# The closing norm of the last 256 rows of a decoder step: its parts moved between VectorE, ScalarE and TensorE

## The chip, the cores and the metric

The kernel runs on one core of one Trainium2 chip. The metric is the device time of one execution in microseconds (us); the median of the runs counts. TensorE (PE) multiplies matrices, VectorE (DVE) and ScalarE (ACT) work element by element, SyncE (SP) issues the transfers (DMA). All matrix results land in PSUM, which has eight banks here; VectorE and ScalarE read them from there.

## The reference, cut to what matters

One layer of a decoder over 528 prompt rows (16 of them learned tokens that are dropped at the end) and 8 sample rows, 2048 columns, float32. The change touches only the last line, the closing norm:

```python
def layer_norm(x, g, b):
    mu = jnp.mean(x, -1, keepdims=True)
    var = jnp.mean(jnp.square(x - mu), -1, keepdims=True)
    return (x - mu) * lax.rsqrt(var + LN_EPS) * g + b
...
    a = silu(h1 @ w_gate) * (h1 @ w_up)
    ff = a @ w_down
    return layer_norm(DEEPNORM_ALPHA * h1 + ff, ln2_g, ln2_b)
```

The outputs of this part are 512 prompt rows (`yp`) and 8 sample rows (`ys`). Weight `ln2_g` and bias `ln2_b` are rows of 2048 values, the same for every row of the output.

## The kernel before, in words

Every weight is split into two float32r parts (`split`, L187 on ScalarE and L188 on VectorE), and every product is three matrix multiplications (`products`, L203, L204, L206). Nearly the whole kernel is such products. The last stage, around which the change lies, holds the residual sum transposed: `acc[m]`, m = 0 to 15, is a tile of 128 columns of the model by 520 rows (8 sample rows, then 512 prompt rows).

The last stage runs over two halves of the rows, h = 0 (sample rows and prompt rows 0 to 255) and h = 1 (prompt rows 256 to 511), and in each over the 16 column tiles m. `down(h, m)` (L1320 to L1333) loads weights (half 0 only, a load for four m at a time, into one of two buffers, L1325), multiplies into a PSUM bank in 12 matrix multiplications, and VectorE adds the bank onto `acc[m]` (L1333). Banks come in turn from a ring of eight.

Class `Rows` (L1338) holds 128 prompt rows; there are four objects, called r0 to r3 below. `Rows.part(q)` (from L1343) runs after each fourth m: TensorE turns four 128x128 tiles into one bank `tz` (L1347), ScalarE copies the bank to a tile `z` of 128 rows by 512 columns (L1349), and VectorE takes its statistics (L1351, for the last quarter from the bank itself). `Rows.end` (from L1354) joins the four statistics (L250), makes the inverse standard deviation with one square root on ScalarE and a Newton step on VectorE (`rstd_of`, L236 to L242), and then makes two passes over each quarter: L1358 subtracts the mean and multiplies by the weight, L1360 multiplies by the inverse deviation and adds the bias, and L1361 sends the quarter out. `ends` hands these passes of r0 and r1 out, one or two per m, during half 1; those of r2 and r3 follow after the last product. `sample_rows` (L1364 to L1409) is the same norm for the 8 sample rows, in six steps put between the products by `next(sample)` in L1411 to L1431; its last step sends 16 small pieces out through SP (L1408).

The order of the instructions on each engine is made by the framework's planner, which simulates the program with its own costs and lets an instruction go when what it needs is there in that simulation; each engine then works off its list in that order. Two helpers bind the planner: `step(engine)`, a block whose instructions on that engine come after those of the `step` block before it, and `tc.high_priority`, used for the weights. In the kernel before, nothing in the last stage stands in a `step` block.

## Time and profile before

| | us |
|---|---|
| median of 3 runs | 1931.51 |
| lowest and highest run | 1930.22, 1931.68 |
| profiled execution: span from its first to its last instruction | 1931.1 |
| TensorE busy in it | 1894.4 (98%) |
| VectorE busy in it | 1539.9 (80%) |
| ScalarE busy in it | 944.1 (49%) |
| granted TensorE clock, mean over the span | 0.992 |

The profile is of one execution, of which the span is the time listed; it lies within the range of the runs and 0.4 us below their median. Times in the rows further down are microseconds from the start of that span; the ones that matter here lie between 1885 and 1931.

### The profile page before, as it was taken

To read this page: it belongs to the slowest core of one execution; us is meant where nothing else is said; L and a number is where in the kernel's file an instruction comes from. 1 tells how busy PE (TensorE), PEld (TensorE's weight loads), DVE (VectorE), ACT (ScalarE), POOL (GpSimd) and SP (SyncE) were. 2 spreads that over 40 slices of the span, in tenths; PEclk is the share of its full clock that TensorE was granted. 3 is DMA by queue.
4 is the path that set the end of the run, shared out by engine and by line. 5 is a ranking of instruction groups with operands and counts; after the bars stand their busy time and mean duration, and the time that the engine had idled before them with its cause. 6 is when DMAs were issued, how large, how long until landed. Compare 5 with 4: busy or idle time off the path is not lost.

```text
span 1931.1 us, 39334 instructions
## 1 busy us (share of the span) xinstructions
PE 1894.4 (98%) x15533; PEld 1865.8 (97%) x15533; DVE 1539.9 (80%) x2734; ACT 944.1 (49%) x1808; POOL 2.7 (0%) x9
## 2 busy tenths in 40 slices
PE   9999999999999999999999999999999999999996
PEld 8999999999989999999999999999999999999996
DVE  6666667768777888888888888888877888888878
ACT  6644445545654544554455555555554444344341
POOL 0000000000000000000000000000000000000000
PEclk9999999999999999999999999999999999999998
DMA  8732222665744555454545445454469664645332
GB/s 276 233 101 66 71 78 75 211 202 193 250 150 164 160 160 172 142 162 158 175 139 178 141 138 165 146 167 145 164 212 356 214 221 162 223 163 202 94 99 89
DMA packets 145241, 319.28 MB, mean 165 GB/s; under 512 B 14288, under 2 KB 66232, under 8 KB 144952
## 3 DMA queue, kind: packets, MB, share of 16 engines
q1 hardware_dynamic: 144480, 315.71, 49.7%
q8 instruction: 122, 2.00, 0.4%
q10 hardware_dynamic: 576, 1.05, 0.2%
q14 instruction: 63, 0.52, 0.1%
HBM read 265.22 MB, written 54.03 MB: 165 GB/s over the span
## 4 chain that ended last, share of the span: by engine, by line
PE 92%; DVE 4%; ACT 2%; DMA 1%; issue 1%; SPq 0%; DVEq 0%; ACTq 0%
PE p_g L203 7%; PE p_g L204 7%; PE p_g L206 7%; PE p_u L203 7%; PE p_u L206 7%; PE p_u L204 7%; PE tri L203 7%; PE tri L206 7%; PE tri L204 7%; PE o L203 3%; PE o L206 3%; PE o L204 3%; PE p_u L996 2%; PE mm_u L203 2%; PE mm_u L206 2%; PE mm_u L204 2%
## 5 line engine op out<-in xcount | busy, mean ns | idle before, releaser
L187 ACT CAST rr<-fr 128x512 fp32r<-128x512 f32 (+1 forms) x1056 | 658.0, 643 | 776.6 <-DVE fr L196 224.0
L188 DVE TENSOR_TENSOR rr<-fr,rr 128x512 fp32r<-128x512 f32 (+1 forms) x1056 | 738.0, 717 | 264.5 <-ACT rr L187 253.2
L196 DVE TENSOR_TENSOR fr<-fr 128x1024 f32<-128x1024 f32 (+1 forms) x304 | 319.7, 1052 | 5.8 <-DMA fr<-in_w_g_dram 5.0
L203 PE MATMUL p_g<-rr 128*128 128x260 f32 x830 | 235.5, 285 | 7.4 <-ACT rr L187 7.1
L206 PE MATMUL p_g<-rr 128*128 128x260 f32 x830 | 230.6, 282 | 0.0
L204 PE MATMUL p_g<-rr 128*128 128x260 f32 x788 | 221.8, 282 | 0.0
L203 PE MATMUL p_u<-rr 128*128 128x260 f32 x770 | 217.5, 283 | 0.2 <-ACT rr L187 0.2
L206 PE MATMUL p_u<-rr 128*128 128x260 f32 x770 | 215.3, 282 | 0.0
L204 PE MATMUL p_u<-rr 128*128 128x260 f32 x748 | 210.6, 282 | 0.0
L206 PE MATMUL tri<-rr 128*128 128x260 f32 x696 | 196.8, 283 | 1.5 <-DVE rr L188 1.5
L203 PE MATMUL tri<-rr 128*128 128x260 f32 x696 | 197.0, 283 | 0.7 <-ACT rr L187 0.7
L204 PE MATMUL tri<-rr 128*128 128x260 f32 x696 | 196.7, 283 | 0.0
L203 PEld LDWEIGHTS p_g<-rr 128*128 128x128 f32 x830 | 156.2, 188 | 9.9 <-ACT rr L187 9.4
L206 PEld LDWEIGHTS p_g<-rr 128*128 128x128 f32 x830 | 155.2, 189 | 0.0
L204 PEld LDWEIGHTS p_g<-rr 128*128 128x128 f32 x788 | 148.1, 188 | 0.0
L203 PE MATMUL o<-rr 128*128 128x260 f32 x512 | 145.0, 284 | 0.3 <-ACT rr L187 0.3
L203 PEld LDWEIGHTS p_u<-rr 128*128 128x128 f32 x770 | 144.9, 188 | 0.3 <-ACT rr L187 0.3
L206 PEld LDWEIGHTS p_u<-rr 128*128 128x128 f32 x770 | 144.6, 189 | 0.0
L204 PE MATMUL o<-rr 128*128 128x260 f32 x512 | 144.1, 282 | 0.0
L206 PE MATMUL o<-rr 128*128 128x260 f32 x512 | 143.6, 282 | 0.2 <-DVE rr L188 0.2
L204 PEld LDWEIGHTS p_u<-rr 128*128 128x128 f32 x748 | 140.6, 188 | 0.0
L206 PEld LDWEIGHTS tri<-rr 128*128 128x128 f32 x696 | 131.3, 189 | 2.2 <-DVE rr L188 2.2
(320 smaller groups left out, 4570.0 us busy)
## 6 DMA issues: line engine op xcount, KB each, us to landing
fr<-in_w_u_dram SPq DMA_DIRECT2D x100, 512.0 KB
fr<-in_w_g_dram SPq DMA_DIRECT2D x90, 512.0 KB
fr<-in_w_d_dram SPq DMA_DIRECT2D x64, 640.0 KB
t_d<-fr SPq DMA_DIRECT2D x140, 260.0 KB
fr<-in_w_o_dram SPq DMA_DIRECT2D x64, 512.0 KB
fr<-in_w_in_dram SPq DMA_DIRECT2D x48, 512.0 KB
rr<-t_d SPq DMA_DIRECT2D x87, 260.0 KB
mid_b<-t_d SPq DMA_DIRECT2D x53, 260.0 KB
```

The costliest lines, as they stand in the source:

```text
L187: nc.scalar.copy(wh, s)
L188: last_lo[0] = (lo or nc.vector).tensor_sub(wl, s, wh.bitcast(F32)).ins
L196: i = op(*args).ins
L203: nc.tensor.matmul(o, wh, hi[j], start=first, stop=False, skip_group_check=onto)
L204: nc.tensor.matmul(o, wh, lo[j], start=False, stop=False, skip_group_check=onto)
L206: nc.tensor.matmul(o, wl, hi[j], start=False, stop=last, skip_group_check=onto)
L996: nc.tensor.matmul(bk, self.q(0, n - 1)[:, k * P:(k + 1) * P], z1[0][4 * (n - 1) + k // 2][:, k % 2, :], start=(k == 0), stop=(k == 7))
```

## The change

For the last 256 rows (r2 and r3, now objects of class `Last`) the norm is rearranged. With s the inverse deviation, the output is z·g·s − mean·s·g + b. For columns 0 to 1535 the product z·g is made as soon as a quarter is there (`Last.scale`), and the rest, −mean·s·g + b, comes from one small TensorE product per quarter (`five`, `lw`, `rows5`: five rows to the product, which are two numbers per row and their low-order parts), and one VectorE pass, after the statistics are known, joins the two. The last quarter keeps its two passes (`centre`, `affine`). The statistics of the first three quarters come from sums that ScalarE accumulates while it copies (`Identity`) and squares (`Square`); only the last quarter keeps `bn_stats`, in two halves. The turning of `acc[m-1]` now stands inside `down(1, m)`, after three of its four groups of products. For r0 and r1, one of two passes per quarter moves to ScalarE (`activation` with scale and bias), and VectorE multiplies and adds. `affine_rows` prepares weight and bias rows for the small products during half 0. The steps of the sample rows come earlier. What follows the last product is bound in `step` blocks. The number of `z` buffers goes from 19 to 16, one for each quarter of r0 to r3, so none is used twice.

```diff
--- before.py
+++ after.py
@@ -47,7 +47,7 @@
 NRAW = 5
 NT = 3
 NG = 56
-NZ = 19
+NZ = 16
 FRW, RRW, MDW = 18960, 24368, 9880
 WIDTH = {"pts": 512, "wh": 512, "wl": 512}
 
@@ -1317,7 +1317,7 @@
     sp[:] = [Pool(rr), KT]
     WIDTH.update(wh=512, wl=512)
 
-    def down(h, m):
+    def down(h, m, mid=None):
 
         if m % 4 == 0 and h == 0:
             pw[h] = plp.tile([P, 4, 4, P], F32, tag="pl", name=f"pl{h}_{m}", bufs=2)
@@ -1330,6 +1330,8 @@
         wh, wl = ws[m]
         for f in range(4):
             products([out], wh[:, f, :], wl[:, f, :], [ah[f][:, hs]], [al_[f][:, hs]], f == 0, f == 3)
+            if f == 2 and mid:
+                mid()
         nc.vector.tensor_add(acc[m][:, hs], acc[m][:, hs], out)
 
     gb = [[pb.tile([P, 512], F32, name=f"gb{i}_{q}") for q in range(4)] for i in range(2)]
@@ -1354,10 +1356,14 @@
         def end(self):
             n = self.n
             mu, r = stats_end(pb, self.st, self.mv, n, f"z{self.c0}")
+            nmr = pb.tile([P, 1], F32, name=f"nmr{self.c0}")[:n]
+            nc.vector.scalar_tensor_tensor(nmr, mu, -1.0, r, op0=ALU.mult, op1=ALU.mult)
+            for z in self.z:
+                nc.scalar.activation(z, z, AF.Identity, scale=r, bias=nmr)
             for q, z in enumerate(self.z):
-                nc.vector.scalar_tensor_tensor(z, z, mu, gb[0][q][:n], op0=ALU.subtract, op1=ALU.mult)
+                nc.vector.tensor_mul(z, z, gb[0][q][:n])
                 yield
-                nc.vector.scalar_tensor_tensor(z, z, r, gb[1][q][:n], op0=ALU.mult, op1=ALU.add)
+                nc.vector.tensor_add(z, z, gb[1][q][:n])
                 nc.sync.dma_start(self.dst[:, q * 512:(q + 1) * 512], z)
                 yield
 
@@ -1408,27 +1414,159 @@
             nc.sync.dma_start(ys[:, m * P:(m + 1) * P], zo[x * NS:(x + 1) * NS])
         yield
 
+    class Last:
+
+        def __init__(self, c0, i, dst):
+            self.c0, self.i, self.dst, self.z = c0, i, dst, []
+            self.st = sts[:, i]
+            self.nc = pb.tile([P, 1], F32, name=f"nc_z{c0}")
+
+        def turn(self, m):
+            q, i = divmod(m, 4)
+            if i == 0:
+                self.tp = bank(f"tz{self.c0}_{q}", 512)
+            nc.tensor.transpose(self.tp[:, i * P:(i + 1) * P], acc[m][:, self.c0:self.c0 + P], ident)
+            if q == 3:
+                if i % 2:
+                    nc.vector.bn_stats(self.st[:, 3 + i // 2, :], self.tp[:, (i - 1) * P:(i + 1) * P])
+            elif i == 3:
+                z = zp.tile([P, 512], F32, tag="z", name=f"z{self.c0}_{q}", bufs=NZ)
+                nc.scalar.activation(z, self.tp, AF.Identity, accum_out=sums[:, self.i, q, 0:1])
+                if q == 0:
+                    nc.scalar.activation(self.nc, sums[:, self.i, 0, 0:1], AF.Copy, scale=-1.0 / 512)
+                nc.scalar.activation(junk, z, AF.Square, bias=self.nc, accum_out=sums[:, self.i, q, 1:2])
+                self.z.append(z)
+
+        def sums_end(self):
+            s1, s2 = [sums[:, self.i, :, k:k + 1] for k in range(2)]
+            d = pb.tile([P, 3, 1], F32, name=f"d_z{self.c0}")
+            both = lambda x: x.to_broadcast([P, 3, 2])
+            nc.vector.tensor_scalar(d, s1, 1.0 / 512, self.nc, op0=ALU.mult, op1=ALU.add)
+            nc.vector.tensor_mul(d, d, d)
+            nc.vector.scalar_tensor_tensor(d, d, -512.0, s2, op0=ALU.mult, op1=ALU.add)
+            nc.vector.tensor_scalar(self.st[:, 0:3, 1::3], both(s1), 1.0 / 512, None, op0=ALU.mult)
+            nc.vector.tensor_scalar(self.st[:, 0:3, 2::3], both(d), 0.5, None, op0=ALU.mult)
+
+        def scale(self, q):
+            nc.vector.tensor_mul(self.z[q], self.z[q], gb[0][q])
+
+    def last_rows(part):
+
+
+        mv = pb.tile([P, 2, 2], F32, name="mv_l")
+        for x in part:
+            nc.vector.bn_aggr(mv[:, x.i, :], x.st.rearrange("p a b -> p (a b)"))
+        mu, var = mv[:, :, 0], mv[:, :, 1]
+        ve, r, t = [pb.tile([P, 2], F32, name=f"{n}_l") for n in ("ve", "r", "t")]
+        zl = [zp.tile([P, 512], F32, tag="z", name=f"z{x.c0}_3", bufs=NZ) for x in part]
+
+        dve = nc.vector
+        wide = lambda a: a.rearrange("p (a b) -> p a b", b=1).to_broadcast([P, 2, 3])
+
+        def centre(x):
+            dve.scalar_tensor_tensor(zl[x.i], x.tp, mu[:, x.i:x.i + 1], gb[0][3], op0=ALU.subtract, op1=ALU.mult)
+
+        def put_out(x, q, z):
+            nc.sync.dma_start(x.dst[:, q * 512:(q + 1) * 512], z)
+
+        def affine(x):
+            with step(dve):
+                dve.scalar_tensor_tensor(zl[x.i], zl[x.i], r[:, x.i:x.i + 1], gb[1][3], op0=ALU.mult, op1=ALU.add)
+            put_out(x, 3, zl[x.i])
+
+        with step(dve):
+            dve.tensor_scalar(ve, var, EPS, None, op0=ALU.add)
+            nc.scalar.activation(t, ve, AF.Sqrt)
+        with step(dve):
+            centre(part[0])
+        with step(dve):
+            dve.reciprocal(r, t)
+            dve.tensor_mul(t, r, r)
+            dve.tensor_mul(t, t, ve)
+            dve.tensor_scalar(t, t, -0.5, 1.5, op0=ALU.mult, op1=ALU.add)
+            dve.tensor_mul(r, r, t)
+        affine(part[0])
+        with step(dve):
+            dve.scalar_tensor_tensor(five[:, :, 0:3], wide(mu), -1.0, wide(r), op0=ALU.mult, op1=ALU.mult)
+        with step(dve):
+            centre(part[1])
+        affine(part[1])
+        tt = bank("five", 2 * P)
+        with step(nc.tensor):
+            for x in part:
+                nc.tensor.transpose(tt[:5, x.i * P:(x.i + 1) * P], five[:, x.i, :], ident)
+        nc.scalar.copy(lh, tt[:5])
+        with step(dve):
+            dve.scalar_tensor_tensor(lw, lh.bitcast(F32), nident[:5, 2:3], tt[:5], op0=ALU.mult, op1=ALU.add)
+
+        pieces = [(x, q) for q in range(3) for x in part]
+        bk = [bank(f"sh{x.i}_{q}", 512) for x, q in pieces]
+
+        for n, (x, q) in enumerate(pieces):
+            with step(nc.tensor):
+                nc.tensor.matmul(bk[n], lw[:, x.i * P:(x.i + 1) * P], rows5[:, q * 512:(q + 1) * 512], start=True, stop=True)
+            with step(dve):
+                dve.scalar_tensor_tensor(x.z[q], x.z[q], r[:, x.i:x.i + 1], bk[n], op0=ALU.mult, op1=ALU.add)
+            put_out(x, q, x.z[q])
+
     sample = sample_rows()
     next(sample)
-    rows = [Rows(NS + P * i, P, yp[P * i:P * (i + 1), :]) for i in range(4)]
-    for h, part in ((0, rows[:2]), (1, rows[2:])):
-        for m in range(KT):
-            down(h, m)
-            if h == 1:
-
-                for _ in range(2 if m % 4 == 1 else 1):
-                    next(ends, None)
-            if h == 0 and m in (1, 2):
-                for i, q in gb_loads[4 * m - 4:4 * m]:
-                    nc.sync.dma_start(gb[i][q], ln2gb[i:i + 1, q * 512:(q + 1) * 512].to_broadcast([P, 512]))
-            if m % 4 == 3:
-                for x in part:
-                    x.part(m // 4)
-            if (h, m) in ((0, 4), (0, KT - 1), (1, 4), (1, 10), (1, KT - 1)):
-                next(sample)
-        ends = chain.from_iterable([x.end() for x in part])
-    for _ in ends:
+    five = pb.tile([P, 2, 5], F32, name="five")
+    nc.gpsimd.memset(five, 1.0)
+    nident = pb.tile([P, 8], F32, name="nident")
+    nc.scalar.activation(nident, ident[:, 0:8], AF.Copy, scale=-1.0)
+    mask = pb.tile([P, 1], F32, name="mask")
+    nc.vector.tensor_add(mask, nident[:, 1:2], nident[:, 4:5])
+    lp = Pool(rr)
+    lh = lp.tile([5, 2 * P], F32R, name="lh")
+    lw = lp.tile([5, 2 * P], F32R, name="lw")
+    rows5 = lp.tile([5, D], F32R, name="rows5")
+
+    def affine_rows(q):
+        sl = slice(q * 512, (q + 1) * 512)
+        g5 = pb.tile([5, 512], F32, name="g5", bufs=1)
+        h5 = lp.tile([5, 512], F32R, name="h5", bufs=1)
+        nc.sync.dma_start(g5[0:3], ln2gb[0:1, sl].to_broadcast([3, 512]))
+        nc.sync.dma_start(g5[3:5], ln2gb[1:2, sl].to_broadcast([2, 512]))
+        nc.scalar.copy(h5, g5)
+        nc.vector.scalar_tensor_tensor(rows5[:, sl], h5.bitcast(F32), mask[:5], g5, op0=ALU.mult, op1=ALU.add)
+
+    sts = pb.tile([P, 2, 5, 6], F32, name="sts")
+    sums = pb.tile([P, 2, 3, 2], F32, name="sums")
+    nc.gpsimd.memset(sts, 256.0)
+    junk = zp.tile([P, 512], F32, name="junk")
+    rows = [Rows(NS + P * i, P, yp[P * i:P * (i + 1), :]) for i in range(2)]
+    last = [Last(NS + P * i, i - 2, yp[P * i:P * (i + 1), :]) for i in (2, 3)]
+    for m in range(KT):
+        down(0, m)
+        if m in (1, 2):
+            for i, q in gb_loads[4 * m - 4:4 * m]:
+                nc.sync.dma_start(gb[i][q], ln2gb[i:i + 1, q * 512:(q + 1) * 512].to_broadcast([P, 512]))
+        if m in (6, 8, 10, 12):
+            affine_rows(m // 2 - 3)
+        if m % 4 == 3:
+            for x in rows:
+                x.part(m // 4)
+        if m in (4, KT - 1):
+            next(sample)
+    ends = chain.from_iterable([x.end() for x in rows])
+    for m in range(KT):
+        down(1, m, lambda: [x.turn(m - 1) for x in last if m])
+        for _ in range(2 if m % 4 == 1 else 1):
+            next(ends, None)
+        if m % 4 == 2 and m > 2:
+            for x in last:
+                x.scale(m // 4 - 1)
+        if m == 14:
+            for x in last:
+                x.sums_end()
+        if m in (3, 7, 11):
+            next(sample)
+    for _ in chain(ends, sample):
         pass
+    for x in last:
+        x.turn(KT - 1)
+    last_rows(last)
 
 
 # ---- launch: one core; the arrays are laid out for the loads, the values are those that come in ----
```

## Rows read from the trace of the kernel before

**Rows 1.** The page, part 1: busy time, share and instructions by engine.
```profile
PE 1894.4 (98%) x15533; PEld 1865.8 (97%) x15533; DVE 1539.9 (80%) x2734; ACT 944.1 (49%) x1808; POOL 2.7 (0%) x9
```
**Rows 2.** Three stretches: us, busy time (instructions) of each engine, granted clock, DMA share, GB/s.
```profile
core 0: us, PE busy (x) PEld busy (x) DVE busy (x) ACT busy (x) POOL busy (x), PEclk, DMA share, GB/s
1885.05:1911.70 26.65, 26.65 (x231) 26.65 (x230) 22.00 (x59) 5.54 (x12) 0.00 (x0) 1.00 0.23 81
1911.70:1915.50 3.80, 1.01 (x10) 0.77 (x8) 3.74 (x12) 2.05 (x4) 0.00 (x0) 0.99 0.00 0
1915.50:1931.10 15.60, 0.45 (x1) 0.18 (x1) 11.88 (x31) 0.67 (x3) 0.00 (x0) 0.50 0.39 139
```
**Rows 3.** Timeline of TensorE at its end: start, busy us, instruction, count [idle before <-releaser].
```profile
1911.33 0.28 PE L206 MATMUL d<-rr 128*128 128x256 f32 x1
1911.45 1.25 PE L1347 MATMUL tz<-fr 128*128 128x128 f32 x10
1915.91 0.45 PE L1403 MATMUL to<-fr 128*128 128x128 f32 x1 [3.21 <-DVE fr L236]
```
**Rows 4.** Timeline of VectorE from the last addition on, and its issues on SP.
```profile
1911.65 0.42 DVE L1333 TENSOR_TENSOR fr<-fr,d 128x256 f32<-128x256 f32 x1 [0.89 <-PE d L206]
...
1915.25 0.38 DVE L250 BATCH_NORM_AGGREGATE fr<-fr 128x2 f32<-128x24 f32 x2
...
1915.74 2.73 DVE L1358 SCALAR_TENSOR_TENSOR mid_c<-mid_c,fr 128x512 f32<-128x512 f32 x4
1918.39 0.14 DVE L236 TENSOR_SCALAR fr<-fr 128x1 f32<-128x1 f32 x1
...
1921.23 0.28 DVE L239 TENSOR_TENSOR fr<-fr 128x1 f32<-128x1 f32 x2
...
1922.00 5.38 DVE L1360 SCALAR_TENSOR_TENSOR mid_c<-mid_c,fr 128x512 f32<-128x512 f32 x8
...
1925.60 2.14 SPq L1361 DMA_DIRECT2D out_dram<-mid_c  x4
```
**Rows 5.** Timeline of VectorE, 1872 to 1877: the unit prices.
```profile
1872.61 1.28 DVE L1351 BATCH_NORM_STATS2 fr<-mid_c 128x6 f32<-128x512 f32 x2
1873.80 0.41 DVE L1333 TENSOR_TENSOR fr<-fr,d 128x264 f32<-128x264 f32 x1
1874.13 1.89 DVE L188 TENSOR_TENSOR rr<-fr,rr 128x512 fp32r<-128x512 f32 x3
1875.94 0.42 DVE L1333 TENSOR_TENSOR fr<-fr,d 128x264 f32<-128x264 f32 x1
```
**Rows 6.** Timeline of VectorE, early in half 1.
```profile
1888.88 0.70 DVE L1351 BATCH_NORM_STATS2 fr<-tz 128x6 f32<-128x512 f32 x1 [1.14 <-ACT mid_c L1349]
...
1891.03 0.10 DVE L236 TENSOR_SCALAR fr<-fr 128x1 f32<-128x1 f32 x1
1891.04 2.73 DVE L1358 SCALAR_TENSOR_TENSOR mid_c<-mid_c,fr 128x512 f32<-128x512 f32 x4
1893.69 0.15 DVE L236 TENSOR_SCALAR fr<-fr 128x1 f32<-128x1 f32 x1
...
1896.39 0.16 DVE L238 RECIPROCAL fr<-fr 128x1 f32<-128x1 f32 x1
...
1897.32 0.15 DVE L238 RECIPROCAL fr<-fr 128x1 f32<-128x1 f32 x1
```
**Rows 7.** ScalarE, groups by line and shape: count, busy us, mean ns, idle before.
```profile
L341 ACT ACTIVATE fr<-fr,mid_a 128x512 f32<-128x512 f32 x16 | 12.1, 805 | 2.5 <-DVE mid_a L336 2.5
L570 ACT ACTIVATION_READ_ACCUMULATOR mid_a<-mid_a,fr 128x1 f32 x64 | 12.0, 187 | 0.0
L1349 ACT COPY mid_c<-tz 128x512 f32<-128x512 f32 x16 | 8.6, 590 | 11.6 <-PE tz L1347 11.6
```
**Rows 8.** ScalarE and SP timelines, weights of the last eight m of half 0.
```profile
1862.16 5.74 SPq L1325 DMA_DIRECT2D fr<-in_w_d_dram  x8
...
1868.86 2.19 ACT L187 CAST rr<-fr 128x512 fp32r<-128x512 f32 x4 [3.14 <-DMA fr<-in_w_d_dram]
```

## The prediction

> **What bounds the kernel now.** I read the page first, then the last stretch in three windows, then the lists of TensorE and VectorE in order of time. The page has TensorE busy for 98% of the span [rows 1], so a change in the last stage is worth only what it does to the end. In the windows [rows 2] the reader is to see three regimes. Up to 1911.7 us TensorE is busy without a gap, but VectorE is busy 22.0 of 26.65 us beside it: it is nearly full too. From 1911.7 on TensorE has ten turns left [rows 3], and VectorE alone sets the end: it is busy 3.74 of 3.80 us, then 11.88 of the last 15.6, and stops at 1927.4 [rows 4] (1922.00 + 5.38). The rest, 1931.1 − 1927.4 = 3.7 us, is the last transfers. So the end is reached when VectorE has worked off its list, and the question is how much work the change takes from that list, and how much waiting it puts in.
>
> **Unit prices on VectorE**, as the distance from one start to the next [rows 5]: statistics of 128x512, 1.19 / 2 = 0.60 us; a product or sum of two 128x512 tiles, 1.81 / 3 = 0.60; the addition of a bank of 256 columns, 0.33. A two-operation pass with a per-row scalar is 2.65 / 4 = 0.66 [rows 6]. A step of the Newton chain that waits for the step before it takes about 0.2: four steps of two instructions each fill 1921.23 to 1922.00 [rows 4], 0.77 / 4 = 0.19.
>
> **r0 and r1 in half 1.** Now: after the mean is known, eight passes of L1358 run at once from 1891.04 while the square root is on its way; the reciprocals come at 1896.39 and 1897.32, behind those passes [rows 6]. In the change both VectorE passes need ScalarE's pass, which needs the inverse deviation. So VectorE has nothing of r0 and r1 to do until: end of the second "add eps", pulled up to about 1891.15, + square root and handing over 0.35 + reciprocal and four steps 1.0 + the negated mean 0.2 + ScalarE's first 128x512 pass, 0.805 [rows 7] (an activation with the same two per-row operands) + 0.2 for hand-overs = **1893.7**. Early bound 1893.0 (no hand-over seen); late bound 1898.5: the reciprocals stay where the planner put them, 1896.39 + 1.2 + 0.8. I take 1893.7, since what held them back, the eight passes, is gone. The passes themselves are 16 x 0.60 instead of 16 x 0.66.
>
> **VectorE from 1893.7 to its last addition.** 16 passes of r0, r1: 9.65. Additions m = 4 to 14: 11 x 0.33 = 3.6. Sample rows, all of them now before the end: three passes of 128x128 and one difference, two sums, six small steps, 1.7 (half of that stood here before). Six weight passes of `scale`: 6 x 0.60 = 3.6. `sums_end`, ten tiny instructions: between 0.7 (0.07 each, packed) and 2.0 (0.2 each, waiting); 1.2, since there is other work to put between. Two half statistics: 2 x 0.33 = 0.7. Removed here are four statistics of 128x512 (2.4), the other four were after the last product. Sum 20.5 us, so the last addition would start at 1893.7 + 20.5 = **1914.2**. Its bank is ready earlier: eight of the ten turns now stand ahead of the last products instead of behind them, 8 x 0.11 = 0.9, so the last multiplication starts at 1911.33 + 0.9 = 1912.2 [rows 3] and the bank is there at 1912.55. VectorE is 1.65 us behind TensorE there; before it was waiting, 0.89 us [rows 4].
>
> **From the last addition to VectorE's end.** Addition 0.42; two turns and hand-overs 0.5; two half statistics 0.66; joining 0.36 [rows 4] (0.38 for two); add eps 0.1; `centre` of r2 0.66, which covers the square root; reciprocal and four steps 1.0; `affine` of r2 0.66; the entries of `five` 0.2; `centre` and `affine` of r3 1.33, which just cover two slow turns of `five` (0.45 each at half clock [rows 2, 3]) and ScalarE's copy; `lw` 0.4; first small product 0.6; six last passes 6 x 0.663 = 3.98. Sum 10.9, against 1927.4 − 1911.65 = 15.75 now. The small products after the first are hidden: 512 columns at the clock of 0.50 that the last window grants are about 0.48 us (four times the 0.12 between the starts of 256 columns at full clock, 1911.33 and 1911.45 [rows 3]), under 0.66. The reads from PSUM cost no more in the rows: statistics from `tz` and from `z` both take 0.69 or 0.70.
>
> **Sum.** 1914.2 + 10.9 = 1925.1 for VectorE, 2.3 before 1927.4; the transfers behind it keep their 3.7, since they again follow passes 0.66 apart. Span 1928.8, and with the 0.4 between the profile's span and the median, **1929.2 us**. As a check by work alone: −4.8 (eight statistics) −10.6 (16 passes) −1.0 (two chains) −1.0 (cheaper passes) + 1.3 + 3.6 + 1.2 + 6.6 (ten passes at the end) + 1.8 (chain, `five`, `lw`) = −2.9, and idle time +2.4 (1.3 early, 1.1 at the end) −1.6 (the gaps of now) gives −2.1.
>
> **Costed at nothing.** ScalarE: eight passes at 0.70 to 0.80, six copies and six squares at 0.6 to 0.8 with 0.19 for each sum [rows 7], some 18 us of the 23 from 1889; the last squares end near 1911, and the joining waits for them only at 1915.4. If that cover goes, each us late is a us. SP: the sample pieces leave earlier, so they no longer stand between the last rows' issues. Half 0: four preparations of 0.6 on ScalarE and 0.66 on VectorE, and eight small loads on SP. Each load but the first pair waits for the preparation before it, and behind it on SP stand the weight loads of 1862.16 [rows 8], the last of which ScalarE already waits for, 3.14 us; TensorE wants that weight at about 1871.8 (eight m of 12 multiplications at 0.12 and 16 turns at 0.11 before half 0 ends at 1885.05); its split is done near 1870.3 (1868.86 plus both parts, some 0.7 each), 1.5 us ahead. Under that, nothing; over it, TensorE stops.
>
> **A bank with two readers.** The row at 1888.88 shows VectorE idle for 1.14 us until ScalarE had copied the same bank, although neither needs the other [rows 6]. In the change the last quarter's four turns and two half statistics share a bank, so the turn of `acc[14]` waits for the first half statistics, with three multiplications of m = 15 behind it. The Trainium skill, "PSUM — Partial Sum Buffer", section "PSUM bank collisions raise a hardware error", says the same as a rule: guard by bank, not by address. By that rule TensorE could stop here, where the change's columns alone would let it go on.
>
> **Rivals.** (1) VectorE is not behind: the planner finds the work room, and the last addition starts at 1912.55. Then 1923.45 + 3.7 + 0.4 = **1927.5**. For it: the idle 0.5 and 0.6 us at the end could take the last `scale` passes, which stand in no `step`. Against it: the list of 20.5 us. (2) The other side: the reciprocals keep their places, the first product comes at 1898.5. Five additions, a sum and a difference fit into the wait (1.7), so the last addition starts at 1898.5 + 18.8 = 1917.3, the end is 1917.3 + 10.9 + 3.7 + 0.4 = **1932.3**, slower. It decides from a first product later than about 1897.5. For it: 5.4 us between L236 and L238 in the list now. (3) The shared bank: if the planner puts the first half statistics last before the addition, at 1914.2, then the two turns and three multiplications and the bank's hand-over come after it, about 1 us: **1930.2**. (4) SP: a preparation load holds the weights up 1.5 us and more; each further us is one, say 3: **1932.2** or above. (5) The change doesn't do what it says: `scale` is made early in the code, but its passes run after the last product. As VectorE's list is full, the sum stays, 1929.2, less up to 1.1.
>
> **Chances.** Forecast 0.47 (with (5)), (1) 0.22, (2) 0.16, (3) 0.08, (4) 0.07. A measurement of this kernel tells 0.2%, 3.9 us, from no change: faster means below 1927.6, slower above 1935.4. (1) lies at that line and the forecast's early edge touches it: 0.20. Slower needs (2) or (4) and more: 0.07. The range leaves out the extremes of (1) and (4): 1926.8 to 1932.9.
>
> **What would show it.** Right: eight of the ten turns stand before the last multiplication; VectorE's first product for r0 at about 1893.7, its last addition late, at 1914 with no wait before it; 10 to 11 us from there to the last pass; 3.7 after. Wrong: a VectorE that waits for TensorE before the last addition (rival 1), a reciprocal beyond 1896 (rival 2), any gap on TensorE between 1870 and 1912 (rivals 3 and 4), or squares on ScalarE after 1914.

## The result and the profile after

The changed kernel takes 1935.12 us, median of 20 runs (1932.08 to 1937.49), against 1931.98 for the kernel before, of which 20 more runs were made beside it: ratio 1.0018, interval 1.0011 to 1.0024. It is 3.1 us slower, where 2.3 us faster was forecast, and above the forecast's range (up to 1932.9). By the bound of 0.2% it is just within no change, but the interval excludes a gain. The profiled execution has a span of 1933.8 us and a time of 1935.58 us; in all runs for which the record has both, the time lies 1.7 to 2.2 us above the span. So the 0.4 us named ahead of the prediction, between the span before and the median of its runs, compares two different measures.

The page, part 1, of the kernel after, answers to [rows 1]:

```profile
PE 1898.9 (98%) x15541; PEld 1866.4 (97%) x15541; DVE 1539.4 (80%) x2743; ACT 955.2 (49%) x1839; POOL 2.9 (0%) x11
```

Nothing is to be seen there: TensorE has 98% in both. The windows of the last stage (columns as in [rows 2]) show it:

```profile
core 0: us, PE busy (x) PEld busy (x) DVE busy (x) ACT busy (x) POOL busy (x), PEclk, DMA share, GB/s
1884.10:1902.90 18.80, 17.38 (x150) 17.14 (x148) 15.02 (x45) 13.37 (x30) 0.00 (x0) 1.00 0.15 58
1902.90:1907.90 5.00, 3.50 (x28) 3.26 (x28) 5.00 (x13) 1.39 (x5) 0.00 (x0) 1.00 0.55 204
1907.90:1910.40 2.50, 0.77 (x4) 0.40 (x4) 2.22 (x15) 1.73 (x5) 0.00 (x0) 0.97 0.03 11
1910.40:1914.30 3.90, 3.85 (x21) 3.85 (x22) 2.28 (x9) 1.21 (x5) 0.00 (x0) 0.58 0.03 6
1914.30:1918.40 4.10, 4.04 (x36) 3.84 (x34) 1.36 (x4) 0.00 (x0) 0.00 (x0) 1.00 0.06 14
```

Before, TensorE was busy without a gap from 1885.05 to 1911.7 [rows 2]. Now it stands for 1.4, 1.5 and 1.7 us of the first three windows. In the fourth it is busy but the granted clock is 0.58, so 21 instructions fill 3.9 us, where 36 fill 4.1 us in the fifth. And VectorE, busy 7.22 of the 7.5 us from 1902.9 to 1910.4, is busy only 2.28 of 3.9 and 1.36 of 4.1 us after that: now it waits for TensorE. The timeline of TensorE names the stops (columns as in [rows 3]):

```profile
1902.96 0.44 PE L1428 MATMUL tz<-fr 128*128 128x128 f32 x2 [1.48 <-DVE fr L1335]
...
1907.98 0.77 PE L1428 MATMUL tz<-fr 128*128 128x128 f32 x4 [1.52 <-DVE fr L1335]
1910.45 0.47 PE L1409 MATMUL to<-fr 128*128 128x128 f32 x1 [1.71 <-DVE fr L1406]
1910.58 0.56 PE L203 MATMUL d<-rr 128*128 128x256 f32 x1
1910.94 0.41 PE L204 MATMUL d<-rr 128*128 128x256 f32 x1
...
1913.50 0.36 PE L204 MATMUL d<-rr 128*128 128x256 f32 x1
1913.69 0.28 PE L206 MATMUL d<-rr 128*128 128x256 f32 x1
```

The third stop is `to`, the turn of the finished sample rows (L1409). It waits for the last of their three passes on VectorE (L1406). Behind it stand the 48 products of m = 12 to 15. Before, the same turn came last of all and waited 3.21 us with nothing behind it [rows 3]. Right after the three stops, 4.7 us together, the products come at a distance of 0.21 us instead of 0.12, from 1910.94 to 1913.50, at the lower of the clock's two levels, 1.2 of 2.4 GHz (granted clock 0.50 in that stretch): 13 x 0.09 = 1.2 us more.

VectorE's timeline, the part that answers to [rows 4, 6]; the first line is half 0's last addition (L1333 before is L1335 now):

```profile
1884.31 0.43 DVE L1335 TENSOR_TENSOR fr<-fr,d 128x264 f32<-128x264 f32 x1 [0.80 <-PE d L206]
...
1890.53 0.33 DVE L238 RECIPROCAL fr<-fr 128x1 f32<-128x1 f32 x2
...
1893.47 1.29 DVE L1364 TENSOR_TENSOR mid_c<-mid_c,fr 128x512 f32<-128x512 f32 x2
...
1910.11 0.28 DVE L1406 TENSOR_TENSOR fr<-fr 128x128 f32<-128x128 f32 x1
...
1913.52 0.42 DVE L1335 TENSOR_TENSOR fr<-fr,d 128x256 f32<-128x256 f32 x1 [1.04 <-PE d L206]
1915.08 0.42 DVE L1335 TENSOR_TENSOR fr<-fr,d 128x256 f32<-128x256 f32 x1 [1.14 <-PE d L206]
1916.72 0.42 DVE L1335 TENSOR_TENSOR fr<-fr,d 128x256 f32<-128x256 f32 x1 [1.22 <-PE d L206]
...
1918.56 0.41 DVE L1335 TENSOR_TENSOR fr<-fr,d 128x256 f32<-128x256 f32 x1
...
1924.44 0.46 DVE L1500 SCALAR_TENSOR_TENSOR rr<-rr,fr,five 5x256 fp32r<-5x256 f32 x1
1925.78 4.04 DVE L1509 SCALAR_TENSOR_TENSOR mid_c<-mid_c,fr,sh 128x512 f32<-128x512 f32 x6 [0.88 <-PE sh L1507]
```

The additions of m = 12 to 14 each wait over a microsecond for their products. So two distances serve to compare the kernels, free of where half 0 happened to end in a profile: **D1**, from the start of half 0's last addition to the start of the last one, and **D2**, from there to the end of VectorE's last pass. In the kernel before, half 0's last addition is the line that follows; half 1's last addition and the last passes are in [rows 4]:

```profile
1885.25 0.43 DVE L1333 TENSOR_TENSOR fr<-fr,d 128x264 f32<-128x264 f32 x1 [0.97 <-PE d L206]
```

Before: D1 = 1911.65 − 1885.25 = 26.40 and D2 = 1927.38 − 1911.65 = 15.73, together 42.13. After: D1 = 1918.56 − 1884.31 = 34.25 and D2 = 1925.78 + 4.04 − 1918.56 = 11.26, together 45.51, which is 3.4 more. The change gives the 4.5 us after the last addition that it is made for, and loses 7.85 ahead of it.

Why the products of m = 12 stand behind `to` is read from TensorE's list as the planner left it. This is a condensed form: `d_12*12` are the twelve products of m = 12 in half 1, `tz_2` turns for the third quarter of r2 and r3, `zm`, `zv` and `to` the sample rows' instructions.

```
before  ... d_10*12 zv*1 d_11*12 tz_2*2 d_12*12 d_13*10 tz_2*2 d_13*2 d_14*12 tz_2*2 d_15*12 tz_2*2 tz_3*8 to*1
after   ... d_9*12 tz_1*2 tz_2*2 d_10*12 d_11*12 tz_2*6 to*1 d_12*12 d_13*12 tz_3*2 d_14*12 d_15*9 tz_3*2 d_15*3 tz_3*4
```

The eight banks are handed out in the order of the code, and in the code the step of the sample rows at m = 11 takes one before `down(1, 12)` does. The theory to be tested: a product can stand no earlier in the list than the first instruction that writes a bank taken before its own. Since `to` needs VectorE's passes and VectorE is behind, TensorE has to stand. Its rivals: the turns moved into `down` stop TensorE (the first two stops are turns); the longer chain of r0 and r1 through ScalarE delays VectorE; the clock, not the stops, takes the time.

### The profile page after: what moved, and what is told of

Same layout as the page of the kernel before. It is cut to its first block, busy times and chain, and to the rows that moved or that the text cites. A ratio compares the mean times of both kernels' runs of the same rounds, so it can differ in the third digit from the quotient of the medians.

```text
span 1933.8 us, 39408 instructions
## 1 busy us (share of the span) xinstructions
PE 1898.9 (98%) x15541; PEld 1866.4 (97%) x15541; DVE 1539.4 (80%) x2743; ACT 955.2 (49%) x1839; POOL 2.9 (0%) x11
## 4 chain that ended last, share of the span: by engine, by line
PE 92%; DVE 4%; ACT 2%; DMA 1%; issue 1%; ACTq 0%; DVEq 0%; SPq 0%
PE p_g L203 8%; PE p_g L204 8%; PE p_g L206 7%; PE p_u L203 7%; PE p_u L206 7%; PE p_u L204 7%; PE tri L203 6%; PE tri L206 6%; PE tri L204 6%; PE o L203 3%; PE o L206 3%; PE o L204 3%; PE p_u L996 2%; PE mm_u L203 2%; PE mm_u L206 2%; PE mm_u L204 2%
```

## The experiments

Every kernel was run in five rounds beside the kernel before, whose medians in the three sets were 1932.19 (e1 to e4), 1932.03 (e5 to e8) and 1931.73 (e9 to e11). All in one table; D1, D2 and their sum are of the profiled execution:

| run | median us | ratio to before, interval | D1 | D2 | sum |
|---|---|---|---|---|---|
| before | 1931.98 | | 26.40 | 15.73 | 42.13 |
| the change | 1935.12 | 1.0018 (1.0011 to 1.0024) | 34.25 | 11.26 | 45.51 |
| e1_sample_late | 1930.05 | 0.9989 (0.9980 to 0.9998) | 29.77 | 11.27 | 41.04 |
| e2_turn_late | 1935.46 | 1.0017 (1.0008 to 1.0026) | 34.22 | 11.26 | 45.48 |
| e3_both_late | 1929.94 | 0.9991 (0.9982 to 1.0000) | 27.82 | 13.37 | 41.19 |
| e4_rows_old | 1933.81 | 1.0012 (1.0003 to 1.0021) | 33.69 | 11.26 | 44.95 |
| e5_claim | 1930.47 | 0.9991 (0.9982 to 1.0000) | 29.80 | 11.26 | 41.06 |
| e6_to_last | 1929.86 | 0.9987 (0.9979 to 0.9996) | 29.61 | 11.27 | 40.88 |
| e7_to_last_turn_late | 1930.82 | 0.9992 (0.9983 to 1.0001) | 27.83 | 13.03 | 40.86 |
| e8_fill | 1937.46 | 1.0030 (1.0018 to 1.0041) | 36.32 | 11.26 | 47.58 |
| e9_before_sample_early | 1938.88 | 1.0041 (1.0027 to 1.0054) | 33.71 | 14.67 | 48.38 |
| e10_to_last_rows_old | 1932.95 | 1.0008 (0.9999 to 1.0017) | 33.68 | 11.24 | 44.92 |
| e11_to_last_pool_scale | 1931.13 | 1.0001 (0.9992 to 1.0010) | 31.09 | 11.33 | 42.42 |

**e1: the steps of the sample rows back where they were in half 1** (m = 4, 10 and after the last product).

```diff
-        if m in (3, 7, 11):
+        if m in (4, 10):
             next(sample)
```

> Only the sample rows' steps in half 1 go back to where they were (after m = 4, m = 10 and after the last product, instead of m = 3, 7, 11). Theory A (order): TensorE stops because turns and the sample rows' last turn stand in its queue ahead of the next products, waiting for VectorE; the stop of 1.71 us before that last turn, and the half clock after it (13 multiplications at 0.21 instead of 0.12, 1.2 us), go: the last product's end comes some 3 us earlier, and the time falls by 2 to 3 us, to about that of the kernel before (ratio 0.9995 to 1.0007). Rival B (load): VectorE has too much to do in half 1 and the stops only show it; the sample rows' work just moves behind the last product, the time stays within 1 us of the change's (ratio 1.0013 to 1.0023).

D1 falls by 4.5 us, and the kernel is 5 us faster than the change and 2 faster than before, more than the 2 to 3 us expected. The last turn now lies right behind the last product and comes at 1913.54 without a stop; ahead of the last product one stop is left on TensorE, at the first turn of a new bank:

```profile
1903.42 0.44 PE L1428 MATMUL tz<-fr 128*128 128x128 f32 x2 [1.66 <-DVE fr L1335]
...
1913.54 0.27 PE L1409 MATMUL to<-fr 128*128 128x128 f32 x1
```

So the sample rows' part of the change carries the loss. This moves three steps at once, though; e6 takes one.

**e2: the turns one m later.**

```diff
-        down(1, m, lambda: [x.turn(m - 1) for x in last if m])
+        down(1, m, lambda: [x.turn(m - 2) for x in last if m > 1])
...
-    for x in last:
-        x.turn(KT - 1)
+    for m in (KT - 2, KT - 1):
+        for x in last:
+            x.turn(m)
```

> Only the turns move: acc[m-2] instead of acc[m-1] is turned inside the products of m, so each addition has one m (1.4 us) more before TensorE wants it. The sample rows stay as in the change. Theory A: the two stops of about 1.5 us for additions shrink to under 0.5 together, the one of 1.7 us for the sample rows stays, the clock may still fall; two more turns come after the last product (0.25 us). Time 1 to 2.5 us under the change's (ratio 1.0005 to 1.0013). Rival B: no change beyond 0.5 us, since VectorE is late by as much as before (ratio 1.0015 to 1.0022).

No difference from the change, in the median or in D1. The expectation of theory A, 1 to 2.5 us less, missed, and the result is what rival B expected. The stops at the turns did not shrink to under 0.5 us together: they are 1.01 and 1.77, and `to` has its stop as before (the record names L1445, which ended last; the sample rows' last pass, L1406, ended just ahead of it):

```profile
1905.08 0.44 PE L1428 MATMUL tz<-fr 128*128 128x128 f32 x2 [1.01 <-DVE fr L1335]
1907.28 0.44 PE L1428 MATMUL tz<-fr 128*128 128x128 f32 x2 [1.77 <-DVE fr L1335]
1909.52 0.45 PE L1409 MATMUL to<-fr 128*128 128x128 f32 x1 [1.80 <-DVE fr L1445]
```

Here the three stops make 4.6 us, in the change 4.7. Turning one m later does not help while `to` stands where it does; that the turns by themselves are not the cost is not shown here but by e5 and e6.

**e3: both edits**, those of e1 and e2.

```diff
-        down(1, m, lambda: [x.turn(m - 1) for x in last if m])
+        down(1, m, lambda: [x.turn(m - 2) for x in last if m > 1])
...
-        if m in (3, 7, 11):
+        if m in (4, 10):
```

> Both moves together. Theory A: no stop over 0.3 us on TensorE in half 1 and no half clock before the last product; the last product ends within 1.5 us of where it does in the kernel before, and the tail behind it, 11.3 us from the last addition to the last pass against 15.7, then shows: 2 to 4 us under the kernel before (ratio 0.998 to 0.999). Rival B: at the change's time less at most 1 us (ratio over 1.001).

D1 is another 2.0 us shorter than in e1, and D2 is 2.1 longer: the same sum. VectorE's work only changes sides. The gain on the kernel before, 2.25 us (1932.19 − 1929.94), is at the low end of the 2 to 4 us expected, and a stop of 0.67 us is left on TensorE at 1904.86, where none over 0.3 was expected. VectorE's list from the last addition on:

```profile
1913.55 0.41 DVE L1335 TENSOR_TENSOR fr<-fr,d 128x256 f32<-128x256 f32 x1
...
1914.76 0.68 DVE L1451 TENSOR_TENSOR mid_c<-mid_c,fr 128x512 f32<-128x512 f32 x1
...
1916.30 0.76 DVE L1431 BATCH_NORM_STATS2 fr<-tz 128x6 f32<-128x256 f32 x2
```

Weight passes and sample passes that stood before the addition now stand between it and the statistics. Once TensorE is out of the way, VectorE's list sets the end, as the prediction had it.

**e4: r0 and r1 as before the change**, both passes on VectorE.

```diff
-            nmr = pb.tile([P, 1], F32, name=f"nmr{self.c0}")[:n]
-            nc.vector.scalar_tensor_tensor(nmr, mu, -1.0, r, op0=ALU.mult, op1=ALU.mult)
-            for z in self.z:
-                nc.scalar.activation(z, z, AF.Identity, scale=r, bias=nmr)
             for q, z in enumerate(self.z):
-                nc.vector.tensor_mul(z, z, gb[0][q][:n])
+                nc.vector.scalar_tensor_tensor(z, z, mu, gb[0][q][:n], op0=ALU.subtract, op1=ALU.mult)
                 yield
-                nc.vector.tensor_add(z, z, gb[1][q][:n])
+                nc.vector.scalar_tensor_tensor(z, z, r, gb[1][q][:n], op0=ALU.mult, op1=ALU.add)
```

> Only the passes of r0 and r1 go back: both on VectorE as scalar-tensor-tensor, none on ScalarE. VectorE then has the 8 first passes to do while the square root is on its way. Theory B (load, made worse by the idle time before ScalarE's passes): VectorE gains some 1 to 1.5 us, stops on TensorE shrink by as much, the time falls by 1 to 1.5 us (ratio 1.0010 to 1.0013). Theory A: VectorE's additions come no earlier where TensorE waits for them, as the passes only stand earlier in the list, and passes of 0.66 instead of 0.60 cost 1 us more; the time stays within 1 us (ratio 1.0013 to 1.0023).

Not conclusive. The median is 1.3 us below the change and the interval overlaps its. `to` does not stop any more, at 1909.02, but two other stops come, each ahead of four turns in a row:

```profile
1894.39 0.97 PE L1424 MATMUL tz<-fr 128*128 128x128 f32 x4 [1.55 <-DVE fr L1335]
...
1903.40 0.97 PE L1424 MATMUL tz<-fr 128*128 128x128 f32 x4 [1.72 <-DVE fr L1335]
```

The edit makes the planner write another list, so it does not isolate the price of ScalarE's part. In this list the rival comes true: the turns, which wait for VectorE's additions, stop TensorE by 3.3 us together, and behind the second of them the granted clock is 0.50 from 1905.15 to 1908.5. What the run says is that undoing this part alone does not remove the loss: D1 is still 33.7.

**e5: the bank of `to` is written early.** One small product that depends on nothing is put between taking the bank and the turn; the turn overwrites it, and nothing reads it.

```diff
         to = bank("to", P)
+        nc.tensor.matmul(to, onesd, onesd, start=True, stop=True)
         nc.tensor.transpose(to, flat(z), ident)
```

> The change with one 128x128 product more, of two constant tiles, written into the bank of the sample rows' last turn just before that turn, which overwrites it. Nothing is taken from VectorE or moved. Theory A, made narrower by the run with the sample rows' steps moved back: the planner hands banks out in the order of the code, so the products of m = 12 can't have one until the sample rows' last turn has taken its own, and that turn takes it only when VectorE has finished the sample rows; the extra product takes the bank without a wait, so the products of m = 12 go ahead of the turn in TensorE's list, and the stop of 1.71 us and the half clock go. Time 3 to 5 us under the change's (ratio to the kernel before 0.9985 to 1.0003). Rival B (VectorE's load): the same list on VectorE, the same time as the change's (ratio 1.0013 to 1.0023).

TensorE's list now reads (the first `to` is the extra product, the second the turn):

```
... d_10*12 d_11*12 to*1 d_12*5 tz_2*2 d_12*7 d_13*12 tz_2*4 tz_3*2 d_14*12 d_15*6 tz_3*2 d_15*6 to*1 tz_3*4
```

The turn has moved behind the last product by itself, and the six turns that stood ahead of it have spread out among the products. On the chip it stands at 1911.09 without a wait, and between 1905 and 1910 TensorE has no gap and the full clock:

```profile
1901.02 0.41 PE L1429 MATMUL tz<-fr 128*128 128x128 f32 x2 [1.57 <-DVE fr L1335]
...
1911.09 0.27 PE L1410 MATMUL to<-fr 128*128 128x128 f32 x1
```

```profile
1905.00:1910.00 5.00, 5.00 (x45) 5.00 (x44) 4.21 (x20) 2.06 (x7) 0.00 (x0) 1.00 0.21 74
```

One instruction more, nothing taken away, and 4.65 us less by the medians. No step was moved here, so it is the taking of the bank that held the products back. This is the run that bears out the theory most directly.

**e6: only the last step of the sample rows goes behind the last product.**

```diff
-        if m in (3, 7, 11):
+        if m in (3, 7):
             next(sample)
```

> Only the sample rows' last step (turn, copy, 16 small transfers) goes behind the last product; their VectorE work stays where the change put it (after m = 3 and m = 7). Theory A: as with the extra product, no stop of 1.7 us, no half clock, 3 to 5 us under the change's time (ratio 0.9985 to 1.0003), and no slower than with all steps moved back, as less of VectorE's work is behind the last product. Rival C, the transfers: the 16 small issues of 5.4 us on SP come between those of the last rows, the end is later by up to 2 us (ratio over 1.0000).

The fastest median: 5.3 us below the change, and faster than before by 0.13%, which is real by its interval and small. The windows and three lines of VectorE:

```profile
1905.00:1910.00 5.00, 5.00 (x45) 5.00 (x44) 4.33 (x20) 1.77 (x6) 0.00 (x0) 1.00 0.30 108
1910.00:1915.00 5.00, 2.58 (x19) 1.94 (x17) 4.62 (x18) 1.48 (x6) 0.00 (x0) 1.00 0.04 7
```

```profile
1891.97 1.29 DVE L1364 TENSOR_TENSOR mid_c<-mid_c,fr 128x512 f32<-128x512 f32 x2
...
1912.41 0.42 DVE L1335 TENSOR_TENSOR fr<-fr,d 128x256 f32<-128x256 f32 x1
...
1919.64 4.04 DVE L1509 SCALAR_TENSOR_TENSOR mid_c<-mid_c,fr,sh 128x512 f32<-128x512 f32 x6 [0.88 <-PE sh L1507]
```

The last addition has no wait before it and TensorE is at full clock up to it. The second and third stop of the change are gone (1.52 + 1.71) and so are the slow products (1.2), 4.4 together; D1 fell by 34.25 − 29.61 = 4.64. The 16 sample pieces now share SP with the last rows again, and D2 is still 11.27, with 3.9 us from VectorE's end to the end of the span (1927.6) against 4.0 in the change: that costs nothing here.

**e7: e6 and the later turns of e2.**

```diff
-        down(1, m, lambda: [x.turn(m - 1) for x in last if m])
+        down(1, m, lambda: [x.turn(m - 2) for x in last if m > 1])
...
-        if m in (3, 7, 11):
+        if m in (3, 7):
```

> The sample rows' last step behind the last product, and the turns one m later. Theory A: the stop of 1.5 to 1.7 us that is left near 1903 (the first turn of a new bank waits for the addition of m = 8, and the products of the next m wait behind it) shrinks below 0.7; VectorE then sets the end, so the gain over the run without the later turns is small: 0 to 1.5 us (ratio 0.998 to 0.9995).

The one stop that e6 keeps (1.58 us, the first turn of a new bank, which waits for an addition) shrinks to 0.67. D1 is 1.8 shorter, D2 1.8 longer, the sum the same within 0.02, and the median 1.0 us higher, with intervals that overlap. TensorE's last stop is not on the path; VectorE's work is.

**e8: is it the stop or the clock?** As e5, but with 32 dummy products, which keep TensorE busy where it stood and leave the products of m = 12 behind `to`.

```diff
         to = bank("to", P)
+        for _ in range(32):
+            nc.tensor.matmul(to, onesd, onesd, start=True, stop=True)
         nc.tensor.transpose(to, flat(z), ident)
```

> The change with 32 products of two constant tiles (128x128) written into the bank of the sample rows' last turn ahead of it, all overwritten by it. They stand in TensorE's list between the additions' turns and that turn, so TensorE works where it stood still; the products of m = 12 still come behind. Theory A with the clock as a part of its own: the granted clock stays at 1.0 through the products of m = 12 and 13 (0.12 each, not 0.21), which gives back about 1.2 us; the filling itself (32 x 0.11 = 3.5 us against 3.2 us of standing still) takes up to 1 us. Time 0 to 1.5 us under the change's (ratio 1.0010 to 1.0018). If the clock has no share, at the change's time or above it (over 1.0018).

Missed in size. A float32 product of 128x128 is two records of 0.11 us each, so the filler is 64 records and 7.2 us, twice what I had reckoned:

```profile
1907.08 1.05 PE L1410 MATMUL to<-fr 128*128 128x128 f32 x8
...
1908.19 3.51 PE L1410 MATMUL to<-fr 128*128 128x128 f32 x30
...
1911.76 3.07 PE L1410 MATMUL to<-fr 128*128 128x128 f32 x26
1914.66 0.28 PE L1411 MATMUL to<-fr 128*128 128x128 f32 x1
1914.89 0.28 PE L204 MATMUL d<-rr 128*128 128x256 f32 x1
```

The clock is 1.00 throughout, and the products that follow come 0.12 apart. From the first instruction behind the products of m = 11 to the turn it is 7.6 us here (1907.08 to 1914.66) and 4.4 in the change (1906.08 to 1910.45): 3.2 more, less the 1.2 of slow products that don't occur, gives 2.0; the sums of D1 and D2 differ by 2.07 and the medians by 2.3. The ratio, 1.0030, lies where no share of the clock was expected (over 1.0018), but that line rested on a filler of half this length. So the share of the clock agrees with the arithmetic and is not shown by itself; a run with a filler of the right length was not made.

**e9: the suspected part alone, in the kernel before.**

```diff
-            if (h, m) in ((0, 4), (0, KT - 1), (1, 4), (1, 10), (1, KT - 1)):
+            if (h, m) in ((0, 4), (0, KT - 1), (1, 3), (1, 7), (1, 11)):
                 next(sample)
```

> The kernel before with one part of the change alone: the sample rows' steps of half 1 after m = 3, 7 and 11 instead of 4, 10 and 15. Theory A (the sample rows' last turn claims its bank ahead of the products of m = 12, and waits for VectorE): TensorE stops before that turn for 1.5 to 4 us, as VectorE is full here too, and what follows runs at half clock for a while; the last product ends 2 to 5 us later, and the time grows by 1 to 5 us (ratio 1.0005 to 1.0025), though the sample rows' work behind the last product is gone. Rival D (the stop comes from the rest of the change, the weight passes and ScalarE's part): no stop over 0.5 us, the time the same or up to 1 us less (ratio 0.9993 to 1.0002).

7.2 us slower than the kernel before, more than the 1 to 5 us expected and more than twice the whole loss of the change. TensorE, and the addition that waits for it:

```profile
1904.31 0.44 PE L1347 MATMUL tz<-fr 128*128 128x128 f32 x2 [1.40 <-DVE fr L1333]
1905.30 0.77 PE L1347 MATMUL tz<-fr 128*128 128x128 f32 x4 [0.56 <-DVE fr L1333]
...
1908.44 0.45 PE L1403 MATMUL to<-fr 128*128 128x128 f32 x1 [2.37 <-DVE fr L1400]
```

```profile
1911.44 0.42 DVE L1333 TENSOR_TENSOR fr<-fr,d 128x256 f32<-128x256 f32 x1 [3.15 <-PE d L206]
```

```profile
1905.00:1910.00 5.00, 2.33 (x12) 1.99 (x13) 3.13 (x11) 1.34 (x3) 0.00 (x0) 0.78 0.29 108
1910.00:1915.00 5.00, 5.00 (x39) 5.00 (x39) 1.26 (x3) 0.00 (x0) 0.00 (x0) 0.88 0.07 15
```

Its list has the same knot, `d_11*12 tz_2*8 to*1 d_12*12`, and the same fall of the clock behind it. D1 grows by 7.31 us and D2 falls by 1.06, as the sample rows' passes no longer stand behind the last addition; together 6.25. Of the 7.31, the three stops shown make 4.3, a fourth at 1896.54 makes 0.4, and the slow products from 1908.5 to 1911.2 make 1.2; the other 1.4 I can't place. Rival D, no such stop, falls. In the change the same knot costs 4.6 (e6) instead of 6.25; why less I have not tried.

**e10: e6 with r0 and r1 as in e4.**

```diff
-        if m in (3, 7, 11):
+        if m in (3, 7):
```

and the diff of e4.

> The sample rows' last step behind the last product, and r0 and r1 with both passes on VectorE as before. If ScalarE's pass for r0 and r1 costs VectorE idle time early in half 1 (some 1.3 us by my sum) and that bounds the end: 0.5 to 1.5 us under the run with the step alone (ratio 0.9979 to 0.9985). If VectorE's longer passes (16 x 0.06) and the later additions weigh as much: within 0.5 us of it (0.9985 to 0.9990).

A miss: 3.1 us slower than e6, D1 33.68. The stops are those of e4, 1.55 and 1.72, each before four turns, at 1891.36 and 1900.36, and the clock between 1900 and 1905 is 0.66. Here too the planner's list is another one, with `tz_1*4 tz_2*2` between the products of m = 9 and 10. By the sums of D1 and D2 the loss against e6 is 4.0 us. TensorE's stops ahead of the last product are 3.3 us against 1.6 in e6, and 16 products 0.21 apart (1901.46 to 1904.66, granted clock 0.50) make about 1.5 more. So with the last step behind, ScalarE's part is worth having, but how much of the loss is VectorE's work and how much the list is not shown. Beside e4 the run says one thing more: the two differ only in the place of the sample rows' last step, and their sums are 44.95 and 44.92. Where `to` does not stop, as in e4, moving it gains nothing.

**e11: e6 with the six weight passes on GpSimd**, to unload VectorE.

```diff
-            nc.vector.tensor_mul(self.z[q], self.z[q], gb[0][q])
+            nc.gpsimd.tensor_mul(self.z[q], self.z[q], gb[0][q])
```

> The sample rows' last step behind the last product, and the six weight passes of the last rows on GpSimd instead of VectorE. If VectorE's list sets the last addition (behind TensorE by some 2 us in the runs without the stop): 1 to 3 us under the run with the step alone (ratio 0.9972 to 0.9982), the last addition within 0.5 us of its bank. If GpSimd's passes slow VectorE's passes beside them, or the sixth ends later than its use at the end: no gain or a loss (ratio 0.9985 or more).

Slower than e6 by 1.3 us, though 3.6 us of work left VectorE. GpSimd's timeline and VectorE's beside it:

```profile
1897.97 7.92 POOL L1451 TENSOR_TENSOR mid_c<-mid_c,fr 128x512 f32<-128x512 f32 x4 [71.21 <-ACT mid_c L1437]
```

```profile
1899.44 0.68 DVE L1366 TENSOR_TENSOR mid_c<-mid_c,fr 128x512 f32<-128x512 f32 x1
...
1900.37 1.43 DVE L1366 TENSOR_TENSOR mid_c<-mid_c,fr 128x512 f32<-128x512 f32 x1
1901.72 1.26 DVE L236 TENSOR_SCALAR fr<-fr 128x8 f32<-128x8 f32 x1
...
1903.23 3.21 DVE L1366 TENSOR_TENSOR mid_c<-mid_c,fr 128x512 f32<-128x512 f32 x2
```

Three of VectorE's own passes of the same shape take 1.4 to 1.6 us instead of 0.6 to 0.7 while GpSimd runs (the one at 1899.44 does not), and a tiny one 1.26 instead of 0.17. The Trainium skill, "SBUF — State Buffer", section "Who interferes with whom", says that a VectorE instruction with two inputs from SBUF contends with a GpSimd instruction that reads SBUF; this trace agrees for the three passes of L1366, which have two such inputs. The tiny one (L236) has one, and why it took so long is not shown. TensorE also has two more stops here than in e6, 1.18 and 0.36 us, at turns that wait for VectorE's additions.

## Why the prediction was wrong, point by point

**The step that failed** is the pair of sentences on the sample rows. The prediction priced them as 1.7 us on VectorE ("Sample rows, all of them now before the end") and, under "Costed at nothing", "SP: the sample pieces leave earlier". Of the step that moved it counted VectorE's passes and SP's transfers, and not its one instruction on TensorE, the turn `to`: that term stood at nothing, without a reason. The instruction waits for VectorE, and the change puts it ahead of the last 48 products. The runs show what the term is: 4.64 us of D1 (e6, the step moved back) and 4.65 us of the median (e5, its bank written early). The row was there: in [rows 3] the same turn waits 3.21 us for VectorE, harmless in last place.

**The assumption under it**, "the bank is there at 1912.55", took TensorE to run on. It held only as long as nothing on TensorE's list needed VectorE's late work. With VectorE 1.65 us behind, by the prediction's own sum, every such instruction makes TensorE wait, and then VectorE waits for TensorE: the two delays add up. The last addition was forecast 1914.2 − 1885.25 = 28.95 after half 0's and came 34.25 after it, 5.3 late. Of these the stops that go with `to` and the clock behind them make 4.4 by rows and 4.64 by e6.

**The rest of the sum held.** VectorE's list from its first product for r0 to its last addition was forecast at 20.5 us; in e6, with the knot untied, it takes 1912.41 − 1891.97 = 20.4, and in the change 1918.56 − 1893.47 = 25.1. D1 in e6 and e5, 29.6 and 29.8, is 0.7 to 0.9 above the forecast of 28.95. That lies ahead of the list: the first product for r0 comes 9.2 us after half 0's last addition in both kernels, where 1893.7 − 1885.25 = 8.45 was forecast. In the change the reciprocals, the four steps and the negated mean fill 1890.53 to 1892.59, 2.06 us with an addition and two instructions of the sample rows between them, where 1.0 + 0.2 were reckoned. D2 in e6 and e5 is 11.27 and 11.26, forecast 10.9. The 0.36 is nearly all in one place: from `lw` to the first last pass 1924.44 to 1925.78, 1.34 us, where 0.4 + 0.6 were reckoned. The transfers behind it took 1933.8 − 1929.82 = 4.0, forecast 3.7. The whole miss of the profiled span adds up: 5.3 + 0.36 + 0.28, less the 0.94 by which half 0 ended earlier in this profile, is 5.0 = 1933.8 − 1928.8. The remaining 0.9 of the median's 5.9 is that it lies 1.3 us above this profile's span, where 0.4 was taken over from before.

**Where the forecast's number had luck.** The medians of e6 and e5, 1929.9 and 1930.5 us, come near the forecast of 1929.2, but partly by chance. Time and span of one execution lie 1.7 to 2.2 us apart, not 0.4; by that distance (an estimate) the execution profiled before took about 1933 us, some 1 us above the median of 20 runs, and the two errors nearly cancel. By D1 and D2, e6 is 42.13 − 40.88 = 1.25 us under the kernel before, where the forecast has 28.95 + 10.9 = 39.85, 2.3 under; the medians of the two differ by 2.2.

**Point by point.** The first product for r0 came at 1893.47, forecast 1893.7, with the reciprocals at 1890.53: rival 2 did not come. (That the two times agree is no more than half 0's earlier end; from there it is the 0.7 late told above.) Rival 4 did not come either: TensorE has no gap from 1856 to 1884.1, and its first stop is at 1901.5. ScalarE's last square ended at 1911.5, forecast near 1911. Of the ten turns that followed the last product before, eight were forecast to go ahead of it; by the list six did, and four are left behind it, a matter of 0.2 us. Rival 1, that VectorE is not behind, was wrong for its reason: in e7 the last addition comes 1.8 us earlier than in e6 and the end does not move, so there VectorE's list sets the end, as argued. Rival 3 was right in kind, TensorE held up in order behind a turn that waits for VectorE, and wrong in the turn and the size: it looked at two turns and three products at the end, about 1 us, and not at a bank taken by a step with 48 products behind it. The Trainium skill, "PSUM — Partial Sum Buffer", section "Engine vs sequencer instructions", says that multiplications start and complete in program order; this trace agrees: the first product of m = 12 starts at 1910.58, behind `to` at 1910.45. The prediction's own test, "any gap on TensorE between 1870 and 1912", is what the trace shows.

**What stays open.** The clock's 1.2 us is read from rows and agrees with e8's arithmetic, but no run isolates it. What ScalarE's part for r0 and r1 is worth alone is not known, as both tries (e4, e10) changed the list. And why the planner's VectorE is ahead of the chip's at m = 11 was not measured.

## What to carry to other kernels

When a step is moved, list its instructions on every engine, and look for one that waited long but at the end of its list: ahead of other work, its wait is paid by all that stands behind it. Where buffers are handed out in code order, the place at which a step takes its bank binds the order as firmly as data do; take the bank when its first writer is ready, or write it early with something that depends on nothing (e5: one small product, 4.65 us). If an engine is a microsecond or two behind by your own sum, then count every other engine's instruction that waits for it as a possible stop.

## What the runs showed of the hardware that was not expected

Three stops of 1.5, 1.5 and 1.7 us, with 3.5 and 0.8 us of work between them, were followed by a clock of 0.58 over 3.9 us; the single stop of 1.6 us in e5 and in e6 was not (1.00 from 1905 to 1910). In e4 and e10, stops of 1.55 and 1.72 us stood 9 us apart; the clock stayed at 1.00 after the first and fell to 0.50 after the second (1905.15 to 1908.5 in e4, 1901.46 to 1904.66 in e10). A float32 product of 128x128 stands as two records of 0.11 us. GpSimd's multiplication of 128x512 took 7.92 / 4 = 1.98 us beside a busy VectorE, and three of VectorE's passes took more than twice their time beside it; the run with six passes moved there was 1.3 us slower than e6 by the medians, with intervals that just overlap.
